# A residual block on one core: the MLP's activations are stored as split pairs, sixteen of its second-half products take seven steps, and the lead is written out

## The chip, the cores and the metric

One core of a Trainium2 chip runs the whole program, one launch. The metric is the device time in microseconds (us), as the median of the runs. The engines are named as in the profile: PE is TensorE (matmuls), DVE is VectorE, ACT is ScalarE, POOL is GpSimd and SP is SyncE, which here only issues loads.

## What is computed

256 rows of 2048 go through one mixer (retention and latent attention, both from the normalised input, merged by gates) and one MLP with a squared ReLU, each with a residual, and a last normalisation. All is float32. Cut to what the change touches:

```python
u = rmsnorm(h, norm_mix_g)
proj = u @ w_in                       # r_q, r_k, r_v, r_g, c_q, c_kv, k_pe, two gates
rq, rk = rope(r_q, positions), rope(r_k, positions) * 128 ** -0.5
...
h = h + merged @ w_out
z = rmsnorm(h, norm_mlp_g) @ w_up     # 256 x 2048 @ 2048 x 8192
h = h + square(relu(z)) @ w_down      # 256 x 8192 @ 8192 x 2048
out = rmsnorm(h, norm_f_g)
```

## The kernel before

**Products.** A float32 operand is split into a high part (ACT casts it, L467) and the rest (DVE subtracts, L468), by `split`; a product takes three matmuls, high by high, high by low, low by high (`Banks.add`, L324 to L326). The weights are loaded (SP), split (ACT, DVE) and used once.

Two shapes do the large products. `Eight` multiplies two blocks of 128 rows of a weight with the two token blocks and two column blocks: 8 products, 24 matmuls of 128x512. `Seven` does the same with 7 products, 21 matmuls, after a scheme of Strassen's: DVE first makes sums of the weight's blocks (`forms`, L286, L295, L296), and the tokens' sums (the "set", four tiles) are made from the activations (`dq`, L1199, L1202, L1203) and split in their turn. At the end of a half the products of the Sevens are combined (`partial`: ACT copies L392 and L394, DVE L388).

**The lead.** The first 45 us load `lead`, 16 rows that hold a part of the input and of six weight tiles, and do the first six projections (`first`, L539 and L541), one row a step. Around it are the loads of `posi` (the positions) and `con` (constants), the input once more by rows (`xn`) for the norm, the rotation angles and tables (`angles`, `table`), the norm's factor (`pb`, `rxb`) and the joining of the two column halves of `first` (`join`). In this part the framework's scheduler orders each engine's instructions; the loads stay in program order. All that comes after runs in the order that the program writes (`manual_schedule`): `stream` takes a list of parts, loads seven parts ahead, prepares (splits) five ahead, and calls `after(n)` behind each part.

**The MLP.** 64 units (`Unit`) make z: a unit is 128 columns of w_up, two parts of 8 matmuls of 128x512 (L170) and 8 of 128x256 (L174). Its result is copied (ACT, L1168) and its halves summed (DVE, L1171, `hs`). Two units make a pair of 256 hidden columns. For each pair `Fresh.step` follows in three steps behind the second unit: relu and square (L1184, L1185) and a store of the 128x512 result to DRAM (`hid`, POOL, L1186); its split, `dd`, and the sums `dq`; the split of the sums, `set`. From unit LAG on, half of a pair's products with the first 1024 columns of w_down follow each unit, all as Sevens, LAG = 5 units behind. When the units are through, the rest of these follow ("the seam"), then the second 1024 columns of w_down for all 32 pairs. There `Hidden` loads a pair back from DRAM (L1234, 256 KB) and splits it anew; the pairs in DS are Sevens, whose sets were kept in SBUF (`combs`), the others Eights. The weights of the last KEPT = 3 pairs are all prepared first and then used one output block after the other, so that the norm of the first blocks lies beside the products of the last. hn2 (the residual) and gt (a gain and a work area) are loaded by POOL at the seam (L1347, L1349).

Of the kernel before, what the change touches and what calls it, by code (L numbers as in the profile page):

```python
# [30 lines left out]
EARLY, LAG = 3, 5  # L31
# [8 lines left out]
DS = 3, 5, 7, 9, 11, 13, 15, 17, 19, 21, 24, 27  # L40
# [59 lines left out]
def block_kernel(ctx: ExitStack, tc: tile.TileContext, A):  # L100
# [163 lines left out]
    class Seven:  # L264
        def __init__(self, banks, src, h, n, end=None):
            self.banks, self.src, self.h, self.j, self.end, self.ws = banks, src, h, n, end, {}
# [143 lines left out]
    def stream(parts, after):  # L410
        loaded = prepped = 0
        for n, (it, h) in enumerate(parts):
            ahead = AHEAD if n else 2
            while loaded < min(len(parts), n + ahead + 3):
                parts[loaded][0].load(parts[loaded][1])
                loaded += 1
            while prepped < min(len(parts), n + ahead + 1):
                parts[prepped][0].prep(parts[prepped][1])
                prepped += 1
            it.mm(h)  # L420
            after(n)
            soon(n)
# [92 lines left out]
    def fetch(out, src):  # L515
        tc.keep_in_program_order(nc.sync.dma_start(out, src))

    for k in range(KT):
# [13 lines left out]
        split(x.hi(k), x.lo(k), t[:, :S], scale=vec0[:, V_MIX + k : V_MIX + k + 1])  # L532
        hi, lo = (wtile(kind, [P, FIRSTS * P]) for kind in ("hi", "lo"))
        step = 3 if k < 2 else FIRSTS
        for j in range(0, FIRSTS, step):
            cs = slice(j * P, (j + step) * P)
            split(hi[:, cs], lo[:, cs], t[:, S:][:, cs])
            for i in range(j, j + step):
                PE.matmul(firsts[i], hi[:, i * P : (i + 1) * P], x.both(k), start=k == 0, stop=False)  # L539
            for i in range(j, j + step):  # L540
                PE.matmul(firsts[i][:, :S], lo[:, i * P : (i + 1) * P], x.hi(k), start=False, stop=k == KT - 1)  # L541

    vec = cp.tile([P, N_VEC], F32, name="vec")
    tc.keep_in_program_order(G.tensor_copy(vec, vec0))
    posf = ip.tile([P, S], F32, name="posf")
    angs = []

    def angles(j):
        ang = ip.tile([P, S], F32, name=f"ang{j}")
        V.tensor_scalar(ang, posf, vec[:, V_INV + j : V_INV + j + 1], None, op0=ALU.mult)  # L550
        kk = ip.tile([P, S], F32, name=f"kk{j}")
        for _ in range(2):
            V.tensor_scalar(kk, ang, INV_2PI, MAGIC, op0=ALU.mult, op1=ALU.add)
            V.tensor_scalar(kk, kk, MAGIC, None, op0=ALU.subtract)
            for cc in (C1, C2, C3):
                V.scalar_tensor_tensor(ang, in0=kk, scalar=-cc, in1=ang, op0=ALU.mult, op1=ALU.add)
        V.tensor_scalar(ang, ang, PI_F, -PI_F, op0=ALU.min, op1=ALU.max)
        V.scalar_tensor_tensor(kk, in0=ang, scalar=-1.0, in1=ang, op0=ALU.mult, op1=ALU.max)
        angs.append((ang, kk))

    V.tensor_copy(posf, posi)
    angles(0)
    angles(1)

    def rms(out, ss, n, width):
        V.tensor_scalar(out, ss, 1.0 / n, EPS, op0=ALU.mult, op1=ALU.add)
        G.tensor_tensor(out=out, in0=out, in1=negh[:, :width], op=ALU.pow)

    early = ip.tile([P, FIRSTS, S], F32, name="early")
    for j in range(FIRSTS):  # L570
        join(early[:, j], firsts[j])
    rx = cp.tile([P, 2], F32, name="rx")
    rms(rx, ssx, D, 2)
    rr = ip.tile([P, 2, P], F32, name="rr")
    for t in range(2):
        V.tensor_scalar(rr[:, t], ones, rx[:, t : t + 1], None, op0=ALU.mult)
    pb = atps("pb")
    for t in range(2):
        PE.matmul(pb[:, t * P : (t + 1) * P], rr[:, t], ident, start=True, stop=True)
    rxb = rope_pool.tile([P, S], F32, tag="rxb", bufs=1, name="rxb")  # L580
    V.tensor_copy(rxb, pb[:, :S])

    tabs = []

    def table(j):
# [70 lines left out]
    def run(parts, after=lambda n: None):  # L656
        with tc.manual_schedule(engines=MANUAL):
            stream(parts, after)
            while later:
                soon(0)  # L660
# [25 lines left out]
    run(product(parts, "rv", A["w_rv"], x, xc, tmp, SEVEN["rv"], tokens(rv, AF.Copy), range(KP)), after)  # L686
# [453 lines left out]
    hid = [hidd.tile([P, 2, S], F32, name=f"hid{i}") for i in range(FT // 2)]  # L1140
    forms = big("forms", shape=(P, 4, 2, 512))

    class Unit:
# [21 lines left out]
        def evict(self):  # L1165
# [3 lines left out]
            if n == 0:  # L1169
                raws[j] = zp.tile([P, 2, S], F32, tag="hs", bufs=3, name=f"hs{j}")  # L1170
# [6 lines left out]
    class Fresh:  # L1177
# [114 lines left out]
    def end(banks):  # L1292
# [6 lines left out]
        d0 = 1 if banks.half else 0  # L1299
# [61 lines left out]
    with tc.manual_schedule(engines=MANUAL):  # L1361
        stream(parts, after)
# [100 lines left out]
```

## Time and profile before

| | |
|---|---|
| median of 3 runs | 1574.44 us (1574.38 to 1576.53) |
| profiled execution | 1574.67 us |
| its span | 1572.9 us, 1.77 us less |
| PE busy | 1553.4 us, 99% |
| DVE busy | 1319.8 us, 84% |
| ACT busy | 965.9 us, 61% |
| POOL busy | 28.4 us, 2% |
| DMA | 325.34 MB, 207 GB/s over the span |

The span runs from the first instruction's start to the last one's end; the time of an execution has a little around that. A row of a timeline has the start, the duration, the engine, the line, the operation, the tiles (out<-in), their shape and the count, and in brackets how long the engine stood idle before and what released it. Matmuls overlap, so their pace is read from the distance of their starts. A row of the windows view has the busy time and the count of PE, its weight loads, DVE, ACT and POOL, then the clock that PE was granted, the share of the DMA engines' time and their rate. A row of the waits view has the total, the count and the longest wait.

### The profile page before, as it was taken

To read this page: it belongs to the slowest core of one execution; us is meant where nothing else is said; L and a number is where in the kernel's file an instruction comes from. 1 tells how busy PE (TensorE), PEld (TensorE's weight loads), DVE (VectorE), ACT (ScalarE), POOL (GpSimd) and SP (SyncE) were. 2 spreads that over 40 slices of the span, in tenths; PEclk is the share of its full clock that TensorE was granted. 3 is DMA by queue.
4 is the path that set the end of the run, shared out by engine and by line. 5 is a ranking of instruction groups with operands and counts; after the bars stand their busy time and mean duration, and the time that the engine had idled before them with its cause. 6 is when DMAs were issued, how large, how long until landed. Compare 5 with 4: busy or idle time off the path is not lost.

```text
span 1572.9 us, 21634 instructions
## 1 busy us (share of the span) xinstructions
PE 1553.4 (99%) x7805; PEld 1318.0 (84%) x7805; DVE 1319.8 (84%) x1835; ACT 965.9 (61%) x1400; POOL 28.4 (2%) x56
## 2 busy tenths in 40 slices
PE   9999999999999999999999999999999999989997
PEld 7888888888898888888888888888888888868886
DVE  7898877899977989976555698888888888899996
ACT  6645655566545667874445566666666666665663
POOL 0000000000000000000000000000000000000000
PEclk9999999999999999999999999999999999999999
DMA  9666655466666654444555766666666667577783
GB/s 317 216 197 205 231 165 162 153 203 210 202 174 226 202 201 140 156 132 168 205 209 190 257 206 216 219 210 224 204 224 201 222 209 220 193 306 250 256 279 114
DMA packets 99884, 325.34 MB, mean 207 GB/s; under 512 B 10432, under 2 KB 11328, under 8 KB 98752
## 3 DMA queue, kind: packets, MB, share of 16 engines
q1 hardware_dynamic: 96784, 310.32, 59.7%
q0 software_dynamic: 2848, 11.54, 1.9%
q10 hardware_dynamic: 144, 2.10, 0.4%
q8 instruction: 61, 1.00, 0.3%
q14 instruction: 47, 0.39, 0.1%
HBM read 311.33 MB, written 12.58 MB: 206 GB/s over the span
## 4 chain that ended last, share of the span: by engine, by line
PE 78%; DVE 2%; ACT 1%; issue 1%; DVEq 0%; POOLq 0%; POOL 0%; ACTq 0%
PE z L170 15%; PE z L174 8%; PE dn L325 6%; PE dn L324 6%; PE dn L326 6%; PE mo L208 2%; PE mo L209 2%; PE mo L211 2%; PE wo L208 2%; PE wo L209 2%; PE wo L211 2%; PE gm L326 2%; PE yr L326 2%; PE yr L324 2%; PE gm L325 2%; PE gm L324 2%
## 5 line engine op out<-in xcount | busy, mean ns | idle before, releaser
L468 DVE TENSOR_TENSOR lo<-raw,hi 128x1024 fp32r<-128x1024 f32 (+3 forms) x235 | 257.2, 1107 | 33.9 <-ACT hi L467 33.4
L163 DVE TENSOR_TENSOR lo<-raw,hi 128x1024 fp32r<-128x1024 f32 (+1 forms) x148 | 173.2, 1172 | 96.5 <-ACT hi L162 96.4
L467 ACT CAST hi<-raw 128x1024 fp32r<-128x1024 f32 (+3 forms) x235 | 221.6, 957 | 51.3 <-PE yr L326 7.0
L162 ACT CAST hi<-raw 128x1024 fp32r<-128x1024 f32 (+1 forms) x148 | 149.6, 1011 | 157.8 <-PE mo L209 44.9
L170 PE MATMUL z<-hT,hi 128*128 128x512 f32 x592 | 147.4, 391 | 0.0
L170 PEld LDWEIGHTS z<-hT,hi 128*128 128x128 f32 x592 | 108.6, 188 | 20.9
L468 DVE TENSOR_TENSOR morelo<-raw,morehi 128x1024 fp32r<-128x1024 f32 (+1 forms) x99 | 107.1, 1096 | 6.3 <-ACT morehi L467 6.3
L170 PE MATMUL z<-hT,morehi 128*128 128x512 f32 x432 | 107.5, 391 | 0.0
L1168 ACT COPY zj<-z 128x512 f32<-128x512 f32 x64 | 37.6, 588 | 107.7 <-PE z L174 107.4
L467 ACT CAST morehi<-raw 128x1024 fp32r<-128x1024 f32 (+1 forms) x99 | 92.1, 946 | 1.4 <-issue 1.0
L170 PEld LDWEIGHTS z<-hT,morehi 128*128 128x128 f32 x432 | 79.3, 188 | 15.3
L174 PEld LDWEIGHTS z<-hT,lo 128*128 128x128 f32 x592 | 80.8, 190 | 5.8
L174 PE MATMUL z<-hT,lo 128*128 128x256 f32 x592 | 82.5, 282 | 0.0
L467 ACT CAST hi<-forms 128x1024 fp32r<-128x1024 f32 x49 | 51.6, 1052 | 40.3 <-DVE forms L286 28.6
L468 DVE TENSOR_TENSOR lo<-forms,hi 128x1024 fp32r<-128x1024 f32 x49 | 59.8, 1221 | 9.2 <-ACT hi L467 8.8
L325 PE MATMUL dn<-lo,dd 128*128 128x512 f32 x166 | 64.9, 391 | 1.1 <-DVE lo L468 1.1
L324 PE MATMUL dn<-hi,dd 128*128 128x512 f32 x166 | 64.8, 390 | 0.0
L326 PE MATMUL dn<-hi,dd 128*128 128x512 f32 x166 | 64.6, 389 | 0.0
L174 PEld LDWEIGHTS z<-hT,morelo 128*128 128x128 f32 x432 | 58.9, 190 | 4.2
L467 ACT CAST morehi<-forms 128x1024 fp32r<-128x1024 f32 x39 | 41.0, 1052 | 33.8 <-DVE forms L286 20.9
L174 PE MATMUL z<-hT,morelo 128*128 128x256 f32 x432 | 60.2, 282 | 0.0
L286 DVE TENSOR_TENSOR forms<-raw,sraw 128x1024 f32<-128x1024 f32 x44 | 53.6, 1218 | 0.0
(478 smaller groups left out, 4034.3 us busy)
## 6 DMA issues: line engine op xcount, KB each, us to landing
raw<-w_up SPq DMA_DIRECT2D x128, 512.0 KB, 4.4
raw<-w_down SPq DMA_DIRECT2D x84, 512.0 KB, 4.0
sraw<-w_down SPq DMA_DIRECT2D x44, 512.0 KB, 5.6
raw<-w_rv SPq DMA_DIRECT2D x32, 512.0 KB, 4.6
raw<-w_rg SPq DMA_DIRECT2D x32, 512.0 KB, 3.9
raw<-w_gret SPq DMA_DIRECT2D x32, 512.0 KB, 4.4
raw<-w_ret_o SPq DMA_DIRECT2D x32, 512.0 KB, 4.8
raw<-w_gmla SPq DMA_DIRECT2D x32, 512.0 KB, 4.3
```

The source lines that it names most:

```text
L162: SC.copy(hi, raw)
L163: V.tensor_tensor(out=lo, in0=raw, in1=hi.bitcast(F32), op=ALU.subtract)
L170: PE.matmul(out, w[0][:, k], x.both(k0 + k), start=start and k == 0, stop=False)
L174: PE.matmul(out[:, :S], w[1][:, k], x.hi(k0 + k), start=False, stop=stop and k == n - 1)
L208: PE.matmul(out, x.hi(k0 + k, ts), w[0][:, k], start=start and k == 0, stop=False)
L209: PE.matmul(out, x.lo(k0 + k, ts), w[0][:, k], start=False, stop=False)
L211: PE.matmul(out, x.hi(k0 + k, ts), w[1][:, k], start=False, stop=stop and k == nk - 1)
L324: PE.matmul(q, ah, wh, start=start, stop=False)
L325: PE.matmul(q, ah, wl, start=False, stop=False)
L326: PE.matmul(q, al, wh, start=False, stop=self.left[f] == 0)
L467: SC.copy(hi, val)
L468: V.tensor_tensor(out=lo, in0=val, in1=hi.bitcast(F32), op=ALU.subtract)
```

## The change

- **Sevens in the second half.** DS has 16 pairs instead of 12. The sets of the first HELD = 12 stay in SBUF; those of pairs 22, 24, 25 and 27 are stored to DRAM (`hset`, POOL) and loaded back (SP).
- **Stored activations.** `hid` now holds the split pair `dd`, 512 KB instead of 256 KB, stored one step later; `Hidden` loads it into `dd` and there is no second split. `dd` has five buffers instead of four, `hs` and `set` two instead of three.
- **LAG** is 3 instead of 5.
- **The seam.** The last pair's Seven calls `end` behind its part 2 instead of 3, and `stream` prepares nothing beyond the first Eight of the second half until the part before the second half.
- **The lead** is in `manual_schedule` now (`lead`): rows are loaded four ahead, posi behind row 6, the input's two halves behind rows 8 and 10, con behind row 12, the angles from step 6 on, two yields a step. What followed the lead (`pb`, tables, joins) is in `settle(n)`, which runs behind the parts n = 0 to 5 of the next product (qk).

As a count of rows in the order of each engine: PE 1404 matmuls of w_down become 1392; DVE and ACT do 32 splits of 128x512 fewer and the sums and splits of four more Sevens; between the lead's end and the MLP's start nothing moves.

```diff
-EARLY, LAG = 3, 5
+EARLY, LAG = 3, 3
...
-DS = 3, 5, 7, 9, 11, 13, 15, 17, 19, 21, 24, 27
+DS = 4, 5, 7, 8, 10, 11, 13, 14, 16, 18, 19, 21, 22, 24, 25, 27
+HELD = 12
...
-            if part == 3 and self.end:
+            if part == self.when and self.end:
...
-    def stream(parts, after):
+    def stream(parts, after, seam=None):
         loaded = prepped = 0
+        until, most = seam or (-1, 0)
         for n, (it, h) in enumerate(parts):
             ahead = AHEAD if n else 2
             while loaded < min(len(parts), n + ahead + 3):
                 parts[loaded][0].load(parts[loaded][1])
                 loaded += 1
-            while prepped < min(len(parts), n + ahead + 1):
+            while prepped < min(len(parts), n + ahead + 1, most if n <= until else len(parts)):
                 parts[prepped][0].prep(parts[prepped][1])
                 prepped += 1
...
+    def row(k):
...
-        if k == 3:
-            fetch(posi, A["positions"].partition_broadcast(P))
-            fetch(con, A["con"])
-        elif k in (7, 11):
-            r = (k - 7) // 4
-            fetch(xn[:, r], A["x"][r * P : (r + 1) * P])
-            SC.activation(xn[:, r], xn[:, r], AF.Square, accum_out=ssx[:, r : r + 1])
...
+    def lead():
+        turning = angles()
+        rows = [row(k) for k in range(4)]
+        G.tensor_copy(vec, vec0)
+        for k in range(KT):
+            t = rows[k]
+            split(x.hi(k), x.lo(k), t[:, :S], scale=vec0[:, V_MIX + k : V_MIX + k + 1])
+            hi, lo = (wtile(kind, [P, FIRSTS * P]) for kind in ("hi", "lo"))
+            step = 3 if k < 2 else FIRSTS
+            for j in range(0, FIRSTS, step):
+                cs = slice(j * P, (j + step) * P)
+                split(hi[:, cs], lo[:, cs], t[:, S:][:, cs])
+                for i in range(j, j + step):
+                    PE.matmul(firsts[i], hi[:, i * P : (i + 1) * P], x.both(k), start=k == 0, stop=False)
+                for i in range(j, j + step):
+                    PE.matmul(firsts[i][:, :S], lo[:, i * P : (i + 1) * P], x.hi(k), start=False, stop=k == KT - 1)
+            if k + 4 < KT:
+                rows.append(row(k + 4))
+            if k == 2:
+                fetch(posi, A["positions"].partition_broadcast(P))
+            elif k in (4, 6):
+                r = (k - 4) // 2
+                fetch(xn[:, r], A["x"][r * P : (r + 1) * P])
+            elif k == 8:
+                fetch(con, A["con"])
+            elif k in (10, 13):
+                r = (k - 10) // 3
+                SC.activation(xn[:, r], xn[:, r], AF.Square, accum_out=ssx[:, r : r + 1])
+            elif k == 15:
+                rms(rx, ssx, D, 2)
+            if k > 5:
+                next(turning, None)
+                next(turning, None)
+        for _ in turning:
+            pass
...
+    def settle(n):
+        if n == 0:
+            for t in range(2):
+                V.tensor_scalar(rr[:, t], ones, rx[:, t : t + 1], None, op0=ALU.mult)
+        elif n == 1:
+            pb = atps("pb")
+            for t in range(2):
+                PE.matmul(pb[:, t * P : (t + 1) * P], rr[:, t], ident, start=True, stop=True)
+            V.tensor_copy(rxb, pb[:, :S])
+        elif n in (2, 3):
+            table(n - 2)
+        elif n == 4:
+            for t in tabs[0]:
+                V.tensor_tensor(out=t, in0=t, in1=rxb, op=ALU.mult)
+        if n < FIRSTS:
+            j = (4, 5, 0, 1, 2, 3)[n]
+            join(early[:, j], firsts[j])
...
-    hid = [hidd.tile([P, 2, S], F32, name=f"hid{i}") for i in range(FT // 2)]
+    hid = [hidd.tile([P, 2, 2, S], F32, name=f"hid{i}") for i in range(DP)]
+    hset = {j: hidd.tile([P, 2, 4, P], F32, name=f"hset{j}") for j in DS[HELD:]}
...
-                G.dma_start(hid[self.j], raw)
-                self.t = hp.tile([P, 2, 2, S], F32R, tag="dd", bufs=4, name=f"dd{self.j}")
+                self.t = hp.tile([P, 2, 2, S], F32R, tag="dd", bufs=5, name=f"dd{self.j}")
-                if self.j in DS:
+                if self.j in DS[:HELD]:
...
-                    self.c = hp.tile([P, 2, 4, P], F32R, tag="set", bufs=3, name=f"set{self.j}")
+                    self.c = hp.tile([P, 2, 4, P], F32R, tag="set", bufs=2, name=f"set{self.j}")
             elif d == 1:
                 split(self.t[:, 0], self.t[:, 1], raw)
+                G.dma_start(hid[self.j], self.t.bitcast(F32))
...
+                if self.j in hset:
+                    G.dma_start(hset[self.j], self.c.bitcast(F32))
...
     class Hidden(Fresh):
-        def __init__(self, j):
-            self.j = j
-            self.c = sets.get(j)
-
         def load(self):
-            self.raw = zp.tile([P, 2, S], F32, tag="hs", bufs=3, name=f"hl{uid[0]}")
-            nc.sync.dma_start(self.raw, hid[self.j])
-
-        def mix(self):
+            self.t = hp.tile([P, 2, 2, S], F32R, tag="dd", bufs=5, name=f"dd{uid[0]}")
+            nc.sync.dma_start(self.t.bitcast(F32), hid[self.j])
             self.c = sets.get(self.j)
-
-        def prep(self):
-            self.t = hp.tile([P, 2, 2, S], F32R, tag="dd", bufs=4, name=f"dd{uid[0]}")
-            split(self.t[:, 0], self.t[:, 1], self.raw)
+            if self.j in hset:
+                self.c = hp.tile([P, 2, 4, P], F32R, tag="set", bufs=2, name=f"set{uid[0]}")
+                nc.sync.dma_start(self.c.bitcast(F32), hset[self.j])
 
...
-        st = Seven(both[0], A["w_down"][0, j], fresh[j], j, last)
+        st = Seven(both[0], A["w_down"][0, j], fresh[j], j, last, 2)
...
-        stream(parts, after)
+        stream(parts, after, (below - 2, below + 2))
```

The three places below show how the change moves instructions; the changed kernel's line numbers are higher than the profile's, by one at first and by more further on. First PE at the start of the MLP, from the second part of unit 3 on (z is a unit's result, hT the transposed input; dn are products of w_down, with the pair 0's dd and set), before:

```order
L170 MATMUL z_8305<-hT_7391,hi_8216 128x512 x8
L174 MATMUL z_8305<-hT_7391,lo_8217 128x256 x8
L170 MATMUL z_8361<-hT_7390,hi_8242 128x512 x8
L174 MATMUL z_8361<-hT_7390,lo_8243 128x256 x8
L170 MATMUL z_8361<-hT_7391,hi_8267 128x512 x8
L174 MATMUL z_8361<-hT_7391,lo_8268 128x256 x8
L170 MATMUL z_8419<-hT_7390,hi_8301 128x512 x8
L174 MATMUL z_8419<-hT_7390,lo_8302 128x256 x8
L170 MATMUL z_8419<-hT_7391,morehi_11_8327 128x512 x8
L174 MATMUL z_8419<-hT_7391,morelo_11_8328 128x256 x8
L324 MATMUL dn_8467<-morehi_12_8355,dd_8294 128x512
L325 MATMUL dn_8467<-morelo_12_8356,dd_8294 128x512
```

and now:

```order
L171 MATMUL z_8307<-hT_7391,hi_8220 128x512 x8
L175 MATMUL z_8307<-hT_7391,lo_8221 128x256 x8
L325 MATMUL dn_8361<-hi_8247,dd_8300 128x512
L326 MATMUL dn_8361<-lo_8248,dd_8300 128x512
L327 MATMUL dn_8361<-hi_8247,dd_8300 128x512
L325 MATMUL dn_8365<-hi_8247,set_8302 128x512
L326 MATMUL dn_8365<-lo_8248,set_8302 128x512
L327 MATMUL dn_8365<-hi_8247,set_8302 128x512
L325 MATMUL dn_8380<-hi_8274,set_8302 128x512
L326 MATMUL dn_8380<-lo_8275,set_8302 128x512
```

Behind unit 3 stood unit 4 (z_8361) and unit 5 (z_8419); now the first product of pair 0 stands there.

Second DVE at the seam, from the last pair's set on (morelo and lo of raw without forms are splits of an Eight's weights, gt from dn the combining of the first half's products), before:

```order
L468 TENSOR_TENSOR lo_13026<-raw_12959,hi_13025 128x512
L468 TENSOR_TENSOR dd_13036<-hl_13009,dd_13036 128x512
L468 TENSOR_TENSOR morelo_256_13040<-raw_13011,morehi_256_13039 128x1024
L468 TENSOR_TENSOR morelo_257_13052<-raw_13023,morehi_257_13051 128x1024
L468 TENSOR_TENSOR dd_13065<-hl_13032,dd_13065 128x512
L468 TENSOR_TENSOR morelo_258_13069<-raw_13034,morehi_258_13068 128x1024
L468 TENSOR_TENSOR lo_13081<-raw_13049,hi_13080 128x1024
L388 TENSOR_TENSOR gt<-dn_8560,gt 128x512
L388 TENSOR_TENSOR gt<-dn_8487,gt 128x512
L468 TENSOR_TENSOR dd_13097<-hl_13061,dd_13097 128x512
L468 TENSOR_TENSOR lo_13101<-raw_13063,hi_13100 128x1024
```

and now:

```order
L470 TENSOR_TENSOR set_12994<-dq_12993,set_12994 128x512
L470 TENSOR_TENSOR lo_13034<-raw_12929,hi_13033 128x512
L470 TENSOR_TENSOR morelo_256_13045<-raw_13013,morehi_256_13044 128x1024
L470 TENSOR_TENSOR morelo_257_13057<-raw_13031,morehi_257_13056 128x1024
L389 TENSOR_TENSOR gt<-dn_8454,gt 128x512
L389 TENSOR_TENSOR gt<-dn_8380,gt 128x512
L470 TENSOR_TENSOR morelo_258_13083<-raw_13042,morehi_258_13082 128x1024
```

Six splits stood between the last piece of the last Seven and gt, four of two Eights' weights and two of stored activations; now the two pieces of one Eight stand there. The last Seven's own weights, which stood between set and lo_13026, are now ahead of set.

Third SP in the lead (each row's load is one of lead, after the first three in pieces), before:

```order
L516 DMA raw_158<-lead 128x1024
L516 DMA raw_178<-lead 128x1024
L516 DMA posi<-positions 128x256
L516 DMA con<-con 128x512
L516 DMA raw_200<-lead 128x1024
L516 DMA raw_220<-lead 128x1024
L516 DMA raw_240<-lead 128x1024
L516 DMA raw_260<-lead 128x1024
L516 DMA xn<-x 128x2048
```

and now:

```order
L518 DMA raw_130<-lead 128x1024
L518 DMA raw_132<-lead 128x1024
L518 DMA raw_155<-lead 128x1024
L518 DMA raw_177<-lead 128x1024
L518 DMA raw_197<-lead 128x1024
L518 DMA posi<-positions 128x256
L518 DMA raw_218<-lead 128x1024
L518 DMA raw_238<-lead 128x1024
L518 DMA xn<-x 128x2048
```

posi and con stood ahead of row 4 (the third raw of the first piece) and the first half of xn behind row 7; now rows 2 to 6 come first, then posi, two more rows and xn, and con comes behind row 12.

More of the change, by code (lines that the diff above doesn't have):

```diff
@@ L264, in block_kernel, with __init__ @@
     class Seven:
-        def __init__(self, banks, src, h, n, end=None):
-            self.banks, self.src, self.h, self.j, self.end, self.ws = banks, src, h, n, end, {}
+        def __init__(self, banks, src, h, n, end=None, when=3):
+            self.banks, self.src, self.h, self.j, self.end, self.when, self.ws = banks, src, h, n, end, when, {}
         def load(self, part):
@@ L515, in fetch, with angles, rms @@
     def fetch(out, src):
-        tc.keep_in_program_order(nc.sync.dma_start(out, src))
-    for k in range(KT):
+        nc.sync.dma_start(out, src)
+    vec = cp.tile([P, N_VEC], F32, name="vec")
+    posf = ip.tile([P, S], F32, name="posf")
+    angs, tabs = [], []
+    def angles():
+        V.tensor_copy(posf, posi)
+        for j in range(2):
+            ang = ip.tile([P, S], F32, name=f"ang{j}")
+            V.tensor_scalar(ang, posf, vec[:, V_INV + j : V_INV + j + 1], None, op0=ALU.mult)
+            kk = ip.tile([P, S], F32, name=f"kk{j}")
+            yield
+            for _ in range(2):
+                V.tensor_scalar(kk, ang, INV_2PI, MAGIC, op0=ALU.mult, op1=ALU.add)
+                V.tensor_scalar(kk, kk, MAGIC, None, op0=ALU.subtract)
+                yield
+                for cc in (C1, C2, C3):
+                    V.scalar_tensor_tensor(ang, in0=kk, scalar=-cc, in1=ang, op0=ALU.mult, op1=ALU.add)
+                    yield
+            V.tensor_scalar(ang, ang, PI_F, -PI_F, op0=ALU.min, op1=ALU.max)
+            V.scalar_tensor_tensor(kk, in0=ang, scalar=-1.0, in1=ang, op0=ALU.mult, op1=ALU.max)
+            angs.append((ang, kk))
+            yield
+    def rms(out, ss, n, width):
+        V.tensor_scalar(out, ss, 1.0 / n, EPS, op0=ALU.mult, op1=ALU.add)
+        G.tensor_tensor(out=out, in0=out, in1=negh[:, :width], op=ALU.pow)
+    rx = cp.tile([P, 2], F32, name="rx")
+    def row(k):
         t = lead0[:, N_VEC:] if k == 0 else wtile("raw", [P, LEAD])
@@ L533, in block_kernel @@
[L533 to L567, printed above, removed]
+        return t
+    def lead():
[33 more added lines that the diff above has]
+            pass
@@ L569, in block_kernel @@
     early = ip.tile([P, FIRSTS, S], F32, name="early")
[L570 to L573, printed above, removed]
     rr = ip.tile([P, 2, P], F32, name="rr")
[L575 to L579, printed above, removed]
     rxb = rope_pool.tile([P, S], F32, tag="rxb", bufs=1, name="rxb")
-    V.tensor_copy(rxb, pb[:, :S])
@@ L583, in block_kernel @@
-    tabs = []
     def table(j):
@@ L654, in tokens, with run @@
         return done
-    def run(parts, after=lambda n: None):
+    def run(parts, after=lambda n: None, before=lambda: None):
         with tc.manual_schedule(engines=MANUAL):
+            before()
             stream(parts, after)
@@ L677, in after @@
         nonlocal making
+        settle(n)
         if n in XC:
@@ L684, in after @@
             rope(qk[:, :, h], early[:, 2 * h : 2 * h + 2], *tabs[0], 64)
-    run(product(parts, "rv", A["w_rv"], x, xc, tmp, SEVEN["rv"], tokens(rv, AF.Copy), range(KP)), after)
+    run(product(parts, "rv", A["w_rv"], x, xc, tmp, SEVEN["rv"], tokens(rv, AF.Copy), range(KP)), after, lead)
     ictx.close()
@@ L1169, in evict @@
             if n == 0:
-                raws[j] = zp.tile([P, 2, S], F32, tag="hs", bufs=3, name=f"hs{j}")
+                raws[j] = zp.tile([P, 2, S], F32, tag="hs", bufs=2, name=f"hs{j}")
             V.tensor_tensor(out=raws[j][:, n], in0=both[:, 0], in1=both[:, 1], op=ALU.add)
@@ L1297, in spread @@
                 fold(banks.half, t, c, banks.rest[t, c])
-        d0 = 1 if banks.half else 0
+        d0 = banks.half
         later.extend([(d0 + 1) * d + d0, lambda: next(sums)] for d in range(2))
```

10 lines of the change are left out of this document (2 added, 8 removed).

## The prediction

> **What bounds the kernel now.** I read the page first, then TensorE's waits, then by timeline the three places that the change edits (the first 45 us, the start of the MLP, the seam between the halves of w_down), and last the second half by windows. The page's span and busy shares:
>
> ```profile
> span 1572.9 us, 21634 instructions
> PE 1553.4 (99%) x7805; PEld 1318.0 (84%) x7805; DVE 1319.8 (84%) x1835; ACT 965.9 (61%) x1400; POOL 28.4 (2%) x56
> ```
>
> TensorE (PE) is the bound: only 19.5 us of the span have no matmul in them. So the change can gain in two ways, by fewer matmuls or by less waiting. The waits of TensorE that lie where the diff is:
>
> ```profile
> PE dn L324 <- ACT gt L392: 2.4, 1, 2.4
> PE dn L325 <- DVE lo L468: 1.9, 2, 1.1
> PE dn L325 <- DVE morelo L468: 0.9, 1, 0.9
> PE first L539 <- ACT hi L467: 0.7, 2, 0.4
> ```
>
> The three dn rows, 5.2 us, are all at the seam; the row of first is the lead. The second half of w_down, in the windows view, with PE, DVE, ACT, clock, DMA share and GB/s:
>
> ```profile
> 1372.20:1545.00 172.80, 167.57 (x732) 137.29 (x731) 170.72 (x195) 113.66 (x147) 1.61 (x3) 0.99 0.78 269
> ```
>
> Here VectorE (DVE) is busy for 170.7 of 172.8 us: two engines are full at once, and DMA is the third. A saved matmul is worth its time only while DVE and the loads keep up. 0.2% of this time is 3.15 us, about what a measurement of this kernel can tell from no change.
>
> All terms are against the profiled execution, 1574.67 us, which is the span and 1.77 us around it; it lies 0.23 us above the median of the runs, 1574.44.
>
> **Lead.** TensorE's rows for steps 2, 10 and 11, and what lies near the end:
>
> ```profile
> 10.62 1.66 PE L539 MATMUL first<-x,hi 128*128 128x512 f32 x6 [0.26 <-ACT hi L467]
> 29.24 1.55 PE L539 MATMUL first<-x,hi 128*128 128x512 f32 x6
> 31.34 1.55 PE L539 MATMUL first<-x,hi 128*128 128x512 f32 x6
> 34.83 0.61 PE L579 MATMUL pb<-con,rr 128*128 128x128 f32 x4
> 35.20 0.96 PE L541 MATMUL first<-x,lo 128*128 128x256 f32 x6
> 41.56 1.07 PE L170 MATMUL qk<-x,hi 128*128 128x512 f32 x4
> 42.47 0.88 PE L541 MATMUL first<-x,lo 128*128 128x256 f32 x6
> 43.18 1.09 PE L170 MATMUL qk<-x,hi 128*128 128x512 f32 x4
> ```
>
> A step takes 31.34 − 29.24 = 2.10 us when nothing is late. The last ends at 43.18, and in front of it stand foreign matmuls, four of qk (42.47 − 41.56 = 0.91) and pb (35.20 − 34.83 = 0.37), which the change puts behind the lead: 43.18 − 1.28 = 41.90 is the end to compare. ACT's rows show why the steps before 29 us are late:
>
> ```profile
> 9.33 0.51 ACT L470 ACTIVATE x<-raw,lead 128x256 fp32r<-128x256 f32 x1 [1.16 <-DMA raw<-lead]
> 14.16 0.51 ACT L470 ACTIVATE x<-raw,lead 128x256 fp32r<-128x256 f32 x1 [2.33 <-DMA raw<-lead]
> ```
>
> Step 2's row lands at 9.33 and nothing in the change brings it sooner. Step 4's lands at 14.16, behind posi and con on SP, and these two move behind it. The big squares of ACT and the angles of DVE go to places where the steps have slack. From step 2 at 10.62, 14 steps of 2.10 end at 40.02: **−1.9** us (−0.5 if a late row remains between, −2.1 if step 2 starts without its wait too). What was beside the lead, pb, tables and joins, now lies in the qk product, which waits for nothing in the trace.
>
> **Start of the MLP.** With LAG 3 the first pair's products follow w_up's unit 3 at once; before, two more units stood between. The rows of before for pair 0 (PE: unit 4 starts, so unit 3 has ended; ACT: a load is awaited; DVE: its subtract, then dd and set of pair 0):
>
> ```profile
> 901.32 2.00 PE L170 MATMUL z<-hT,hi 128*128 128x512 f32 x8
> 893.46 1.05 ACT L467 CAST hi<-raw 128x1024 fp32r<-128x1024 f32 x1 [2.52 <-DMA raw<-w_up]
> 894.54 1.23 DVE L468 TENSOR_TENSOR lo<-raw,hi 128x1024 fp32r<-128x1024 f32 x1 [2.94 <-ACT hi L467]
> 900.08 0.68 DVE L468 TENSOR_TENSOR dd<-hs,dd 128x512 fp32r<-128x512 f32 x1
> 903.14 0.69 DVE L468 TENSOR_TENSOR set<-dq,set 128x512 fp32r<-128x512 f32 x1
> ```
>
> Even in the old order dd was done at 900.7 and set at 903.75; PE had 11.1 us more. Now DVE has ahead of dd, in place of two subtracts of w_up (2.3 us), the pair's weights: a sum and two subtracts of 128x1024 (1.13 each from start to start) and two short sums (1.33 together), 4.7 us. That is 2.4 more, of which I let 1.1 be taken from DVE's idle time ahead of them: dd at 902.0, and set 3.06 behind it as before, 905.1; its hi half about 903.7. PE does one matmul at 901.32, waits 0.45 for dd, does two, waits 1.2 for set's hi, does two, waits 1.0 for its lo: **+2.7** us, a wait that before didn't have (+1 if more of the idle time is used; +3.5 if none). Behind the waiting matmuls on PE stand the rest of the pair's products and unit 4; ACT's copy of unit 4 and DVE's sum come later by as much, and nobody is short of those, so the wait is paid once and not won back: the stage is PE's.
>
> **Seam.** w_up's last unit ends when dn starts, at 1374.56 (call it t0); these are PE's row there, DVE's and ACT's rows of the last pair, and PE's first product of the second half:
>
> ```profile
> 1374.56 0.40 PE L324 MATMUL dn<-morehi,dd 128*128 128x512 f32 x1
> 1375.44 0.43 DVE L1171 TENSOR_TENSOR hs<-zj 128x256 f32<-128x256 f32 x1 [0.71 <-ACT zj L1168]
> 1380.52 0.68 DVE L468 TENSOR_TENSOR dd<-hs,dd 128x512 fp32r<-128x512 f32 x1
> 1382.22 0.62 ACT L467 CAST set<-dq 128x512 fp32r<-128x512 f32 x1 [1.67 <-DVE dq L1203]
> 1383.24 0.68 DVE L468 TENSOR_TENSOR set<-dq,set 128x512 fp32r<-128x512 f32 x1
> 1395.15 0.77 PE L324 MATMUL dn<-morehi,dd 128*128 128x512 f32 x1 [2.36 <-ACT gt L392]
> 1395.15:1398.50 3.35, 3.35 (x8) 2.63 (x9) 3.31 (x5) 3.35 (x5) 0.00 (x0) 0.51 1.00 380
> ```
>
> A matmul of this form follows the last after 0.2267 us: 72 of them between these two rows.
>
> ```profile
> 1405.05 0.39 PE L324 MATMUL dn<-hi,dd 128*128 128x512 f32 x1
> 1421.37 0.39 PE L324 MATMUL dn<-hi,dd 128*128 128x512 f32 x1
> ```
>
> Before, 63 matmuls (14.28 us) stand between t0 and the second half, which starts at t0 + 20.59: 6.3 us lost, by the waits and the slow first matmuls after each. Now 42 stand there (9.52). DVE's order from hs to set is the same row for row in kinds and sizes, so dd is there at t0 + 6.6, set's hi at 8.3, its lo at 9.4. PE reaches the last pair after 21 matmuls, at 4.8, does one, waits 1.5 for dd, does two, waits 1.4, does two, waits 0.6: 3.5 us lost, and the second half starts at t0 + 13.05. The 2.36 for gt goes, since the sums start a part sooner and DVE and ACT hold no weights of the next pairs ahead of them; its next-latest is the second 128x1024 piece of pair 0, done at about 12.2. **−2.8** us (−4.5 if the three waits are half as long, +1 if the sums still come as late).
>
> **The clock.** The clock row shows half rate for 3.35 us after the 2.36 wait, and the waits of 0.9 to 1.1 before it brought none (the window's 0.99 over 172.8 us is 1.7 us, this one stretch). Eight matmuls at half rate cost 8 × 0.2267 = 1.8. In the changed kernel the three waits at the seam put 2.9 us of idle time in 3.4, more than the 2.36, and those at the start of the MLP 2.65 in 3.8, also more. I take one halving for the two places, as there is one now: 0. Both would be +1.8, none −1.8. [...]
>
> **Four more Sevens.** 24 − 21 = 3 matmuls fewer for each, 12 × 0.2267 = **−2.7** us.
>
> **Second half.** In the first half the stores on POOL double, 8.4 MB more in the 473 us from 901 to 1374, and the splits leave nothing on PE's path there: 0. Behind the seam, DVE's rows for a Seven, a stored pair's split, and an Eight:
>
> ```profile
> 1450.19 1.22 DVE L286 TENSOR_TENSOR forms<-raw,sraw 128x1024 f32<-128x1024 f32 x1
> 1456.82 0.69 DVE L468 TENSOR_TENSOR dd<-hl,dd 128x512 fp32r<-128x512 f32 x1
> 1457.42 1.22 DVE L468 TENSOR_TENSOR lo<-raw,hi 128x1024 fp32r<-128x1024 f32 x1
> 1459.69 0.68 DVE L468 TENSOR_TENSOR dd<-hl,dd 128x512 fp32r<-128x512 f32 x1
> 1460.29 1.22 DVE L286 TENSOR_TENSOR forms<-raw,sraw 128x1024 f32<-128x1024 f32 x1
> 1547.47 2.73 DVE L1253 SCALAR_TENSOR_TENSOR hn<-gt,rh,hn 128x512 f32<-128x512 f32 x4
> 1546.54 0.39 PE L324 MATMUL dn<-over,dd 128*128 128x512 f32 x1
> ```
>
> Seven 6.63 (1450.19 to 1456.82), Eight 2.27, split 0.60. The 32 splits that go take 19.2 us off DVE, the four Sevens in place of Eights put 4 × 4.36 = 17.4 on, and one pair's weights (6.63) are now prepared ahead of t0: DVE is done with the last weights at t0 + 172.9 − 8.4 = 164.5 instead of 172.9 (1547.47). PE starts the last pass 7.54 + 2.72 sooner than now (1546.54), at t0 + 161.7, and wants the last weights 15 matmuls on, at 165.1. So DVE's margin at the end falls from 2.5 us to 0.6, and two Sevens and an Eight in a row take DVE 15.5 where PE needs 66 matmuls, 15.0. Any delay of DVE now counts. I take **+0.8** (0 to +3).
>
> Sum: −1.9 + 2.7 − 2.8 − 2.7 + 0.8 = −3.9: profiled 1570.8, and as a median 0.23 lower, **1570.6 us**.
>
> **Rivals.**
> *DMA becomes the bound of the second half (slower).* The window above moved 269 × 172.8 = 46.5 MB. The stored pairs grow from 256 to 512 KB (32 × 0.262 = 8.4 MB) and four sets of 0.52 MB are added: 57.0 MB, in 172.8 − 10.3 = 162.5 us, 351 GB/s. These two windows stand on either side of that:
>
> ```profile
> 1398.00:1408.00 10.00, 10.00 (x45) 8.21 (x44) 9.93 (x14) 2.63 (x4) 0.00 (x0) 0.97 1.01 386
> 1510.00:1530.00 20.00, 20.00 (x90) 16.54 (x90) 19.87 (x23) 12.38 (x15) 0.00 (x0) 1.00 0.96 314
> ```
>
> At 386 the loads need 148 us and nothing happens, at 314 they need 182. Midway between 314 and the window's 269/0.78 = 345, at 330, they need 173: 10 us late in place of my 0.8: 1580. From 335 GB/s down (7.9 late) it is slower than before by over 0.2%. For: at 314 the share already stood at 0.96. Against: in the other window loads of the same kinds went at 386, and the loads are issued seven parts ahead. Chance 0.18.
> *The clock halves at both places.* +1.8: 1572.4, within 0.2%. Chance 0.15.
> *DVE is the bound of the second half.* There are seven runs of two Sevens and an Eight, each 0.57 over PE, 4.0 in all; the lone Seven with its Eight (8.9 against 10.2) gives 1.3 back. If the 0.6 margin is all there is, 2.1 in place of 0.8, and with a wait for the cast at each (DVE stands idle 2.1 of 172.8 now) 3: 1572.8, within 0.2%. Chance 0.15.
> *The clock halves nowhere.* −1.8 at the seam, of which DVE, then 1.2 us late at the end, gives 1.2 back: 1570.0, faster. [...] Chance 0.10.
> My forecast has the rest, 0.42.
>
> **How the numbers follow.** Faster: 0.42 + 0.10 = 0.52; same: 0.15 + 0.15 = 0.30; slower 0.18. Downward, a quicker start of the MLP (+1) and a quicker seam (−4.5) would together bring 1567.2; upward the range takes in both rivals at 1572.8 and part of the DMA's, to 1578. The forecast's own range is 1567 to 1571.5.
>
> **What would show it.** Right: the lead's last step ends near 40; waits of TensorE for dd and set behind unit 3 of about 2.7; the second half starts 13 us after w_up's last unit, without the wait for gt; hardly a wait of TensorE after that. Wrong: no wait at the MLP's start, waits of DVE or ACT for dd, sraw or raw loads in the second half with the DMA share at 1, or TensorE waiting for DVE from one Seven to the next.

## The result: slower, 1579.21 us against 1574.47

The changed kernel takes 1579.21 us as the median of seven runs (1578.26 to 1582.88), the kernel before 1574.47: a ratio of 1.0035, 95% interval 1.0023 to 1.0046. The forecast was 1570.6, range 1567 to 1578. The profiled execution is the longest of the seven, 1582.88 us, so the sums below explain a little more than the median has. Its page and the waits of TensorE on products of w_down (line, released by: total, count, longest):

```profile
span 1581.1 us, 21563 instructions
PE 1557.5 (99%) x7793; PEld 1317.6 (83%) x7793; DVE 1319.0 (83%) x1823; ACT 956.4 (60%) x1376; POOL 30.2 (2%) x60
```

```profile
PE dn L326 <- DVE morelo L470: 2.6, 5, 0.8
PE dn L325 <- ACT set L469: 2.3, 2, 1.1
PE dn L326 <- DVE over L470: 1.8, 2, 1.1
PE dn L327 <- DVE dd L470: 1.3, 1, 1.3
PE dn L326 <- DVE lo L470: 1.0, 2, 0.8
PE dn L327 <- DVE set L470: 1.0, 2, 0.7
PE dn L325 <- ACT over L469: 0.5, 1, 0.5
```

The wait for gt is gone; waits for dd and set are there as forecast, and others (morelo, lo, over) that were not. Where they lie shows by TensorE's rows: the end of the lead, the first pair's products and the unit behind them, the seam with the second half's first product (1396.61), and the first and last product of the last pass (1549.20 and 1571.95).

```profile
40.20 2.03 PE L171 MATMUL qk<-x,hi 128*128 128x512 f32 x8
899.73 0.40 PE L325 MATMUL dn<-hi,dd 128*128 128x512 f32 x1
902.13 0.50 PE L325 MATMUL dn<-hi,set 128*128 128x512 f32 x1 [1.14 <-ACT set L469]
903.56 0.79 PE L327 MATMUL dn<-hi,set 128*128 128x512 f32 x1 [0.69 <-DVE set L470]
906.61 2.00 PE L171 MATMUL z<-hT,hi 128*128 128x512 f32 x8
1381.88 0.40 PE L325 MATMUL dn<-hi,dd 128*128 128x512 f32 x1
1388.57 0.49 PE L327 MATMUL dn<-hi,dd 128*128 128x512 f32 x1 [1.29 <-DVE dd L470]
1390.21 0.50 PE L325 MATMUL dn<-hi,set 128*128 128x512 f32 x1 [1.14 <-ACT set L469]
1396.61 0.39 PE L325 MATMUL dn<-morehi,dd 128*128 128x512 f32 x1
1549.20 0.39 PE L325 MATMUL dn<-over,dd 128*128 128x512 f32 x1
1557.14 0.80 PE L326 MATMUL dn<-over,dd 128*128 128x512 f32 x1 [1.08 <-DVE over L470]
1571.95 0.39 PE L327 MATMUL dn<-over,dd 128*128 128x512 f32 x1
```

Against the rows of before, at 0.2267 us a matmul:

| place | forecast | measured | from |
|---|---|---|---|
| lead, kept to unit 3's end | −1.9 | −1.6 | 899.73 against 901.32 |
| start of the MLP | +2.7 | +4.2 | 899.73 to 906.61 for 12 matmuls (2.7) |
| seam and the clock there | −2.8 | −2.8 | 14.73 for 42 matmuls (9.52), 5.2 lost; before 6.3, and 1.7 by half clock behind it |
| four more Sevens | −2.7 | −2.7 | 12 matmuls |
| second half up to the last pass | +0.8, with the last pass | +5.7 | 152.59 for 648 matmuls (146.9) |
| last pass | in the +0.8 | +6.7 | 22.75 for 71 spacings (16.1) |
| behind the last matmul | 0 | −1.1 | 1581.1 − 1571.95 = 9.15, before 1572.9 − 1562.63 = 10.27 |

The sum is +8.4, the spans differ by 8.2. All that went wrong lies in the second half, 12.4 us where I had 0.8, and 1.5 at the MLP's start.

**Behind the seam.** Two windows of the changed kernel (PE, weight loads, DVE, ACT, POOL, clock, DMA share, GB/s), then POOL's, SP's and ACT's rows around them:

```profile
1385.00:1390.00 5.00, 2.78 (x12) 1.74 (x10) 4.90 (x9) 2.84 (x4) 0.91 (x2) 1.00 0.31 124
1400.00:1405.00 5.00, 5.00 (x24) 4.13 (x22) 0.50 (x1) 0.76 (x1) 0.00 (x0) 1.00 1.01 386
```

```profile
1389.08 0.53 POOL L1225 DMA_DIRECT2D hid<-dd  x1 [17.49 <-DVE dq L1227]
1389.62 0.55 POOL L1370 DMA_DIRECT2D hn<-hnkeep  x1
1390.17 0.54 POOL L1372 DMA_DIRECT2D gt<-norm_f_g  x1
...
1382.57 0.33 SPq L1260 DMA_DIRECT2D dd<-hid  x1
1391.87 1.46 SPq L356 DMA_DIRECT2D raw<-w_down  x2
...
1404.24 1.05 ACT L469 CAST hi<-raw 128x1024 fp32r<-128x1024 f32 x1 [7.06 <-DMA raw<-w_down]
```

The last pair's store now waits for dd (the row names dq, the sums that DVE does right behind it), and hn2 and gt stand behind it on POOL: they start at 1389.6, 7.7 us behind t0 (1381.88). In the 5 us ahead of that the DMA share is 0.31, in the later window 1.01; the weights that SP asks for from 1391.87 on are loaded in the same stretch as these 3 MB, which land 9.4 (hn2) and 13.8 us (gt) after their issue, ACT waits 7.06 us for one, and DVE, which has no time to give, does 0.5 us of work in 5. TensorE has work left until 1423 and then catches up with DVE: waits and slow starts of 5.3 us until 1475.

**The last pass.** SP's row of waits between 1535 and 1546 (for a free raw buffer), then SP's, ACT's and DVE's rows for the last weights:

```profile
SPq L356 <- DVE lo L470: 7.1, 3, 6.1
```

```profile
1543.63 1.46 SPq L356 DMA_DIRECT2D raw<-w_down  x2
...
1549.85 1.05 ACT L469 CAST morehi<-raw 128x1024 fp32r<-128x1024 f32 x1 [2.57 <-DMA raw<-w_down]
1552.32 1.05 ACT L469 CAST over<-raw 128x1024 fp32r<-128x1024 f32 x1 [1.42 <-DMA raw<-w_down]
...
1550.93 1.23 DVE L470 TENSOR_TENSOR morelo<-raw,morehi 128x1024 fp32r<-128x1024 f32 x1 [2.02 <-ACT morehi L469]
1553.40 1.22 DVE L470 TENSOR_TENSOR over<-raw,over 128x1024 fp32r<-128x1024 f32 x1 [1.24 <-ACT over L469]
```

Then a window with the last loads in it and one of the first part of the pass (the clock is the third number from the right):

```profile
1541.00:1552.00 11.00, 10.63 (x47) 8.46 (x46) 8.46 (x9) 5.87 (x7) 0.00 (x0) 1.00 0.82 292
1555.00:1560.00 5.00, 3.92 (x10) 2.60 (x9) 4.96 (x8) 0.00 (x0) 0.00 (x0) 0.50 0.00 0
```

The weights of the kept pairs land later than TensorE wants them, it waits 2.9 us in pieces, and the clock stands at half for 6.8 us, from 1555.0 to 1561.8. SP waits up to 6.1 us for DVE to free a buffer; the load that it asks for at 1543.63 is cast at 1552.32, 8.7 us later, and DVE, which frees the buffers, stands idle 2.0 and 1.2 us for these casts. The loads run at 292 GB/s and a share of 0.82 there, not at the 386 of the window above.

### The profile page after: what moved, and what is told of

Read it like the earlier page. It is cut to its first block, busy times and chain, and to the rows that moved or that the text cites. A ratio compares the mean times of both kernels' runs of the same rounds, so it can differ in the third digit from the quotient of the medians.

```text
span 1581.1 us, 21563 instructions
## 1 busy us (share of the span) xinstructions
PE 1557.5 (99%) x7793; PEld 1317.6 (83%) x7793; DVE 1319.0 (83%) x1823; ACT 956.4 (60%) x1376; POOL 30.2 (2%) x60
## 4 chain that ended last, share of the span: by engine, by line
PE 70%; DVE 6%; DMA 2%; issue 2%; ACT 2%; DVEq 0%; POOLq 0%; POOL 0%; SPq 0%; ACTq 0%
PE z L171 14%; PE z L175 7%; PE dn L326 4%; PE dn L327 4%; PE dn L325 4%; DMA raw<-w_down 2%; PE mo L209 2%; PE mo L210 2%; PE mo L212 2%; PE wo L210 2%; PE wo L209 2%; PE wo L212 2%; PE gm L327 2%; PE yr L327 2%; PE yr L325 2%
## 5 line engine op out<-in xcount | busy, mean ns | idle before, releaser
L470 DVE TENSOR_TENSOR lo<-raw,hi 128x1024 fp32r<-128x1024 f32 (+3 forms) x234 | 253.5, 1098 | 34.7 <-ACT hi L469 33.6
L469 ACT CAST hi<-raw 128x1024 fp32r<-128x1024 f32 (+3 forms) x234 | 218.3, 949 | 56.4 <-DMA raw<-w_down 10.1
L470 DVE TENSOR_TENSOR morelo<-raw,morehi 128x1024 fp32r<-128x1024 f32 (+1 forms) x96 | 103.3, 1092 | 8.5 <-ACT morehi L469 8.4
L469 ACT CAST morehi<-raw 128x1024 fp32r<-128x1024 f32 (+1 forms) x96 | 88.7, 942 | 4.2 <-DMA raw<-w_down 2.8
L469 ACT CAST hi<-forms 128x1024 fp32r<-128x1024 f32 x53 | 55.7, 1050 | 41.5 <-DVE forms L287 28.9
L470 DVE TENSOR_TENSOR lo<-forms,hi 128x1024 fp32r<-128x1024 f32 x53 | 64.7, 1221 | 8.8 <-ACT hi L469 8.3
L469 ACT CAST morehi<-forms 128x1024 fp32r<-128x1024 f32 x43 | 45.2, 1051 | 33.7 <-DVE forms L287 20.8
L327 PE MATMUL dn<-hi,dd 128*128 128x512 f32 x153 | 59.9, 392 | 1.4 <-DVE dd L470 1.3
L287 DVE TENSOR_TENSOR forms<-raw,sraw 128x1024 f32<-128x1024 f32 x48 | 58.4, 1217 | 2.1 <-DMA raw<-w_down 2.1
L326 PE MATMUL dn<-lo,dd 128*128 128x512 f32 x153 | 60.1, 393 | 0.0
L325 PE MATMUL dn<-hi,dd 128*128 128x512 f32 x153 | 60.0, 392 | 0.0
```

The costliest lines, as they stand in the source:

```text
L325: PE.matmul(q, ah, wh, start=start, stop=False)
L326: PE.matmul(q, ah, wl, start=False, stop=False)
L327: PE.matmul(q, al, wh, start=False, stop=self.left[f] == 0)
L469: SC.copy(hi, val)
L470: V.tensor_tensor(out=lo, in0=val, in1=hi.bitcast(F32), op=ALU.subtract)
```

## The experiments

Two theories at first. Q: the loads come late because they stand behind a wait on the engine that issues them, and then in one burst. B: the prediction's rival, 57 MB are too many for the second half wherever they start.

**1. hn2 and gt sooner** (ahead of the last pair's store on POOL).

```diff
-        if n == above:
+        if n == above - 3:
```

> The changed kernel, with the 3 MB of hn2 and gt issued by POOL three parts sooner, ahead of the last pair's store. Theory Q (queues: the loads are late because they stand behind a wait in an in-order queue, and then come in one burst): the two loads start at the end of w_up's last unit, about 7 us sooner, in a stretch where the DMA share is 0.3 to 0.5; ACT's wait for raw of 7.1 us falls under 3, DVE's idle 4.8 us under 1.5, PE's 5.3 us of waits between 1423 and 1475 mostly go: 1574 to 1576 us. Theory B (bandwidth: 57 MB are too many for the second half, wherever they start): the wait moves to a later load and the time stays within 1.5 us of 1579.2.

1574.74 us (11 runs; ratio to before 1.0006, 0.9997 to 1.0015), 4.5 below the changed kernel. POOL's rows and ACT's longest wait for a weight at that place:

```profile
1378.74 0.54 POOL L1370 DMA_DIRECT2D hn<-hnkeep  x1 [8.22 <-PE z L175]
1381.27 0.54 POOL L1372 DMA_DIRECT2D gt<-norm_f_g  x1 [1.99 <-PE z L175]
1387.73 0.54 POOL L1225 DMA_DIRECT2D hid<-dd  x1 [5.92 <-DVE dd L470]
...
1397.24 1.06 ACT L469 CAST hi<-raw 128x1024 fp32r<-128x1024 f32 x1 [1.18 <-DMA raw<-w_down]
```

The 7.06 is 1.18, and the lost time between the seam and the last pass is 0.8 us instead of 5.7. SP asks for that weight 10.0 us behind t0 in both kernels (here at 1390.79, with t0 at 1380.80), so what moved is the 3 MB. The bytes are the same: B falls here, Q holds. The last pass still loses 4.6 us. (Lost time is counted from start to start here, as in the table; some expectations have it 0.1 or 0.2 lower.)

**2. No hold at the seam.**

```diff
-        stream(parts, after, (below - 2, below + 2))
+        stream(parts, after)
```

> The changed kernel without the hold at the seam: weights of the second half are prepared five parts ahead again. Theory Q, if the hold is what blocks the loads (their buffers stay full until the weights in them are split): loads go out while DMA is idle at 1382 to 1392 and the 7.1 us wait of ACT shrinks to under 3, but TensorE waits for the sums (gt) again, 1 to 2.5 us: 1576 to 1578 us. If only hn2 and gt matter: ACT still waits 5 us or more and the time is 1579 to 1582. Theory B: 1579 or more.

1580.30 us (5 runs; 1.0036, 1.0023 to 1.0048), as the changed kernel. ACT still waits 8.4 us for one weight: the hold is not what makes the loads late. TensorE doesn't wait for gt without it either, so nothing of the gain at the seam hangs on it in this order.

**3. The sets' loads on POOL.** On SP they wait for a free set buffer, and all later loads with them (in the changed kernel SP starts none between 1508.91 and 1517.07):

```profile
SPq L1264 <- PE dn L327: 13.5, 2, 7.8
```

```diff
-                nc.sync.dma_start(self.c.bitcast(F32), hset[self.j])
+                G.dma_start(self.c.bitcast(F32), hset[self.j])
```

> The changed kernel with the four loads of stored sets issued by POOL instead of SP, so that their wait for a free set buffer (7.8 and 5.7 us on SP) holds up nothing else. Theory Q: the DMA share has no hole at 1510 to 1520 any more, the last weights land 5 us or more sooner, TensorE's waits for over and morelo in the last pass (2.9 us) and the half clock there (about 3.1 us) go: 1573 to 1575.5 us. Theory B: the bytes are the same, no change beyond 1.5 us.

1582.69 us (5 runs; 1.0052, 1.0039 to 1.0065), 3.5 above the changed kernel's median, though the two intervals against before overlap. The last pass loses 3.0 us instead of 6.7; its waits are only 0.6 shorter (2.3 against 2.9), the rest is the clock, which stays at 1.00 there. ACT's waits for weights over the half grew:

```profile
ACT hi L469 <- DMA raw<-w_down: 13.6, 4, 7.6
```

In the changed kernel that row has 10.1. My expectation was wrong: this wait on the queue is long, but moving the loads off it gains nothing. Why the waits behind the seam grew, the run doesn't show.

**4. The second half of before**, with the lead, the lag and the seam of the change.

```diff
-DS = 4, 5, 7, 8, 10, 11, 13, 14, 16, 18, 19, 21, 22, 24, 25, 27
+DS = 3, 5, 7, 9, 11, 13, 15, 17, 19, 21, 24, 27
...
+                G.dma_start(hid[self.j], raw)
...
-                G.dma_start(hid[self.j], self.t.bitcast(F32))
```

`Hidden` loads 256 KB and splits again, and the buffers are those of before.

> The lead, LAG 3, the hold and the earlier sums of the change, but the second half of before: 12 Sevens, stored activations in 256 KB, split again, no stored sets. Both theories: lead -1.6, start of the MLP +4.1 (waits 2.6 and the half clock), seam -1 to -3, second half 0: 1573 to 1575.5 us. If the hold at the seam alone makes the loads late, this one is slower, 1577 or more, since hn2 and gt and the weights then collide here too.

1575.36 us (11 runs; 1.0005, 0.9996 to 1.0014). Its last pass loses nothing, the start of the MLP 4.2 us, and two waits for ACT 34 us behind t0 another 1.75. So the last pass is the work of the new second half, and lag and seam by themselves give no gain: what the seam and the lead save, the MLP's start and these waits take.

**5. Experiments 1 and 3 together.**

> hn2 and gt sooner, as in the first experiment, and the set loads on POOL as in the third. Theory Q: each repairs one place, the first the waits of 41 to 94 us behind the seam (5.3), the second part of the last pass (its 4.5 of lost time to 2.9 or less): 1571 to 1573.5 us. Theory B: the third experiment was slower than the changed kernel by 3.5 us because four more loads come sooner and crowd the others, and it does so here: 1576 or more.

1575.31 us (11 runs; 1.0011, 1.0002 to 1.0020): no better than the first alone. Theory Q holds for hn2 and gt and not for the sets.

**6. Experiment 1, and the first half steps behind unit 4.**

```diff
-        if i >= LAG:
+        if i == 4:
+            halfstep(0)
+            halfstep(1)
+        elif i > 4:
             halfstep(i - LAG)
```

> hn2 and gt sooner, and the first two half steps of w_down behind w_up's unit 4 instead of units 3 and 4 (LAG stays 3 from there on). If the start of the MLP costs what the trace shows (waits of 2.6 us and eight matmuls or so at half clock, 3.4 in the first experiment's trace), it goes whole, since pair 0's set then has 5.5 us more: 3 to 4 us under the first experiment, 1571 to 1572. If the wait only moves to unit 5 or into the steps behind it: less than 1 us.

1571.84 us (11 runs; 0.9981, 0.9973 to 0.9990), 2.9 below the first. From the first product to the next unit there is no lost time left (0.03 us; in the first experiment 3.4). The wait was a matter of one unit's time.

**7. Experiments 5 and 6 together.**

> All three edits: hn2 and gt sooner, set loads on POOL, first half steps behind unit 4. Theory Q: they add up, 1567.5 to 1570 us, below the kernel before by 0.3% or more. Theory B: 1573 or more.

1571.33 us (8 runs; 0.9978, 0.9968 to 0.9988), the same as the sixth and between the two expectations. The last pass still loses 6.2 us in the sixth and 4.4 in this one; the sixth's rows of waits there:

```profile
PE dn L326 <- DVE over L470: 2.2, 2, 1.5
PE dn L325 <- ACT over L469: 0.4, 1, 0.4
```

**8. The lead alone**, in the kernel before.

> Before, with only the lead of the change. The trace of the changed kernel has the lead 1.7 us shorter; with nothing else moved this should be kept to the end: 1572.6 to 1573.2 us. If the stages behind the lead give it back (the joins and tables now beside the qk product): 1574 to 1575.

1571.75 us (11 runs; 0.9983, 0.9974 to 0.9991), 2.7 below before and more than I expected. 1.6 of it is there at the end of the lead and stays to the last matmul (1561.00 against 1562.63); 0.9 lies behind it, where the last stores land (9.4 against 10.27 from the last matmul to the end). What shortens those, no run shows; all kernels with the new lead have it.

**9. Two pairs kept.** A third theory, L: the demand is too high at one place. The last four pairs are Eights and three of them are kept. An Eight brings 1.57 MB (two weights and the stored pair), 4.1 us at 385 GB/s, for 2.3 us of DVE's work, so by this estimate, from the 386 of the window behind the seam, DMA sets the pace there: 16 us for the four. TensorE has 14.3 us of work over them, a Seven, an Eight and 18 matmuls. In before an Eight brought 1.31 MB, 3.4 us. D is the prediction's other rival, that DVE is too slow over the whole half.

```diff
-KEPT = 3
+KEPT = 2
```

on the sixth experiment.

> The sixth experiment (hn2 and gt sooner, first half steps behind unit 4) with two pairs kept for the last pass instead of three. Theory L (local demand at the end: the last four Eights need 1.57 MB each for 2.3 us of DVE work and, three of them kept, have only 14 us of TensorE's work to land 6.3 MB, 16 us at 385 GB/s): with two kept there are 18 us, the waits for over and morelo (3 us) and the half clock after them (3 us) go, 1566 to 1569 us. Theory D (DVE itself is too slow over the whole half, by the 0.6 us of margin in the prediction): DVE ends as late as before and the waits stay, 1571 to 1573.

1566.20 us (5 runs; 0.9947, 0.9933 to 0.9960): 5.6 below the sixth and 8.4 below before. The waits of TensorE for products of w_down that are left, and ACT's row for the same weight as above:

```profile
PE dn L327 <- DVE dd L470: 1.3, 1, 1.3
PE dn L325 <- ACT set L469: 1.1, 1, 1.1
PE dn L327 <- DVE set L470: 0.4, 1, 0.4
PE dn L326 <- DVE morelo L470: 0.2, 1, 0.2
```

```profile
1540.98 1.05 ACT L469 CAST over<-raw 128x1024 fp32r<-128x1024 f32 x1 [1.41 <-DMA raw<-w_down]
```

The load is as late as in the sixth, where ACT waits 1.42 for it, but the pass starts at 1544.65 instead of 1538.89 and finds its weights ready. DVE has the same work, and up to the last pass the half loses 0.9 us: D, as a shortage of DVE over the whole half, falls. That the end was late by the loads this run alone doesn't show, since a pass that starts 5.8 us later forgives a late DVE as well; what speaks for the loads is DVE's idle time ahead of the last weights, above for the changed kernel and 1.1 and 1.2 us in the sixth.

**10. Twelve Sevens** (the sixth, three kept).

```diff
-DS = 4, 5, 7, 8, 10, 11, 13, 14, 16, 18, 19, 21, 22, 24, 25, 27
+DS = 4, 5, 7, 8, 10, 11, 13, 14, 16, 18, 19, 21
```

> The sixth experiment with the first 12 of the 16 Sevens only, so that no set is stored or loaded, 2.1 MB less, and DVE has 17 us less to do. TensorE has 12 matmuls, 2.7 us, more. Theory D: the waits in the last pass go, 6 us, and it comes to 1568 to 1569.5. Theory L: the last Eights are more in number, 11 in a row, each 4.1 us of DMA against 5.4 of TensorE, and DVE is far ahead, so that the loads are asked for in time: also 1568 to 1570; what tells the two apart is the run with two kept pairs. If Sevens with stored sets pay as they stand: 1573 or more.

1568.96 us (5 runs; 0.9963, 0.9951 to 0.9976). No wait in the last pass, though it has three kept pairs of 512 KB too: the large loads at the end, theory L, aren't enough by themselves. What is gone here is 17 us of DVE's work, with 2.1 MB of sets. Against the ninth it is 2.8 longer, the 12 matmuls (2.72), so the four Sevens with stored sets bring about that once the last pass isn't late; with three kept they lose 2.9.

**11 and 12. Two pairs kept in the changed kernel, and in the kernel before.**

> The changed kernel as it is, with two pairs kept instead of three and nothing else. Theory L: the lost time of the last pass (6.5 us) goes, that behind the seam (5.3) and at the start of the MLP (4.2) stays: 1573 to 1575 us. If the last pass was only late because the seam had made DVE late (one cause for both): DVE is still late and 2 us or less come back, 1577 or more.

> The kernel before with two pairs kept, as a control. In its trace no wait lies in the last pass, so theory L has nothing to win here: 1574 to 1576 us, a little up if less of the last norm is hidden. If two kept pairs are better in themselves, by the end of the program: 1572.5 or less.

1574.55 us (11 runs; 1.0002, 0.9994 to 1.0011) and 1574.26 us (11 runs; 1.0001, 0.9992 to 1.0010). In the changed kernel the edit brings 4.7 us, though the half up to the last pass still loses 5.1 us (5.7 in the changed kernel), by the same waits for DVE:

```profile
PE dn L326 <- DVE morelo L470: 1.9, 4, 0.8
```

The later start of the pass would have hidden a lateness left over from the seam too. That the last pass has a cause of its own is shown by experiments 1 and 6, where the waits behind the seam are gone or small and it still loses 4.6 and 6.2 us. In the kernel before the edit brings nothing: it is no gain in itself, it repairs what the change broke.

## Why the prediction was wrong

- **Second half, "I take +0.8 (0 to +3)": the step that failed.** It measured 12.4. The sum of DVE's work against TensorE's was right: with the same work the ninth experiment loses 0.9 us there. What I left out is when the loads start. I costed the longer stores on POOL at "0", and looked only at the first half; at the seam the last of them, moved behind dd, stands ahead of hn2 and gt. Moving these two took 4.5 us off (experiment 1).
- **The last pass, in the same term.** I compared when DVE is done and when TensorE wants the last weights, and no more. With DVE's margin used up, buffers come free late (SP waits up to 6.1 us for one), and the last weights are asked for too late for their own transfer (8.7 us from there to the cast). Experiments 9 and 11 took 5.6 and 4.7 us off. How much of it is the size of the stored pairs, and how much the four Sevens more, stays open: no run has sixteen Sevens with pairs of 256 KB.
- **The DMA rival** (0.18, 1580) had the time, by luck, and the wrong reason. It weighed all bytes against the whole half. The ninth experiment moves the same bytes and is 13 us faster. What counted were two places.
- **The DVE rival** had 2.1 to 3 us over the whole half. As a steady loss it falls with the ninth experiment too (0.9); that DVE has hardly a margin at the end was right, and without that the last loads were not late (experiment 10).
- **Start of the MLP, +2.7.** The mechanism was right (waits for dd and set behind unit 3); it measured 4.2, since the clock halved there as well in this trace, and 2.9 us came back in experiment 6.
- **The clock: one halving for two places.** There were three:

```profile
903.50:906.70 3.20, 3.14 (x8) 2.52 (x9) 3.04 (x6) 2.67 (x5) 0.32 (x1) 0.53 0.85 220
1391.00:1395.00 4.00, 3.70 (x10) 2.93 (x11) 3.11 (x4) 2.37 (x4) 0.00 (x0) 0.57 0.92 299
```

  and the last pass, above. Some 28 matmuls start 0.43 us apart instead of 0.23, about 5.6 us, where before had 1.7: the term that I set to 0 is some 4 us of the places above. At the three falls lie waits of 1.14 and 0.69 us, of 1.29, 1.14 and 0.36, and of 0.58, 0.48 and 0.76, with a few matmuls between them: none of them is an unbroken gap like the 2.36 us in before.
- **Lead, seam, Sevens** held: −1.6, −2.8 and −2.7 against −1.9, −2.8 and −2.7. The ninth experiment has them all and hardly any of the new waits.

## What to carry to other kernels

When a store is moved to a later step, look at what stands behind it on its queue at the one place where that queue matters, not at its bytes. When the engine that prepares data gets just enough time, check the stretch where the bytes for a unit of its work are largest, with the transfer's own time and the number of buffers, and not the mean over the stage. A scheme with fewer matmuls was worth about its matmuls (2.8 us against 2.7), but only after the loads at its two ends had been set right.

## What the runs showed of the hardware that was not expected

The wait of 2.4 us for gt is followed by half clock in the trace of before (from 1395.20 to 1398.61; matmuls start 0.43 us apart), and in that of the lead alone the same wait is not (its row of waits, and two windows, one with the wait in it and one behind it, with the clock at 1.00; matmuls start 0.23 us apart):

```profile
PE dn L325 <- ACT gt L393: 2.4, 1, 2.4
```

```profile
1390.00:1395.00 5.00, 2.64 (x12) 1.68 (x10) 5.00 (x6) 5.00 (x8) 0.00 (x0) 1.00 0.78 253
1395.00:1400.00 5.00, 4.29 (x19) 3.29 (x19) 4.93 (x8) 2.68 (x4) 0.00 (x0) 1.00 0.95 331
```

In the changed kernel's trace the clock falls at 903.07, 1391.17 and 1555.01 and rises 3.41, 3.42 and 6.83 us later. The three waits at the seam (1.29, 1.14 and 0.36) are followed by half clock there, and in experiment 2 the same three (1.29, 1.14 and 0.35) are not, in a window of the same times as the one above:

```profile
1391.00:1395.00 4.00, 3.65 (x17) 3.00 (x17) 4.00 (x5) 4.00 (x6) 0.00 (x0) 1.00 0.97 317
```

So the same waits cost more in one trace than in another: half clock behind the wait for gt cost 1.7 us in before and nothing in the lead alone. What sets the two apart, these runs don't show.

The changed kernel's runs spread over 4.6 us, those of the ninth and the tenth experiment, with the fewest waits, over 1.3 and 0.7.
